# A fused attention and recurrence layer on one core: the score products as 32-row strips of four heads, without the copies that stacked them

## The chip, the cores and the metric

The kernel runs on one core of a Trainium2 chip. The time is device microseconds of one execution, the median of several runs. A second, profiled execution gives the span from the first to the last instruction and the rows that are quoted. "PE" is the matrix engine (TensorE), "PEld" its loads of stationary weights, DVE, ACT and POOL are the vector, scalar and GpSimd engines, and SP is the engine whose queue issues nearly all transfers (SPq in rows).

## The reference

512 tokens of 1024 features go through one layer. A vector `c` gives shift, scale and gate; then

```
h    = rmsnorm(x) * (1 + scale) + shift
proj = h @ w_in                       # q, k, v, z_attn, x_lru, z_lru
q, k = rope(q), rope(k)               # 8 heads of 64
s    = (q @ k.T) / 8, causal          # MoBA: 2 blocks of 256, top 3, so all past blocks are kept
attn = softmax(s) @ v
rec  = rg_lru(causal_conv(x_lru))     # recurrence over time
y    = [rmsnorm(attn) * silu(z_attn), rmsnorm(rec) * silu(z_lru)] @ w_out
out  = rmsnorm(x + gate * y) * final_gain
```

Everything is float32. The kernel gets near that accuracy with operands split into a rounded high part and a low part (`hi`, `lo`, type fp32r) and three products: hi·hi, hi·lo and lo·hi.

## The kernel before

**Order.** The whole program is written as a list of operations (`op`), each with an engine, an estimated cost, the tiles it reads and writes, and a due time. `Plan.emit` (line 97) simulates the engines with these estimates, picks the next operation of each engine, and so fixes one order for each engine and for SP's transfer queue. On the chip each engine runs its order as it stands: an instruction whose input is late holds up all that stand behind it on that engine. Tiles come from pools of `N2` buffers of 2 KB per partition, `N4` of 4 KB and `N8` of 8 KB (line 182) and from 8 banks of PSUM, of which at most 6 are given to `"side"` work at a time (scores, transposes, gates); a load waits until a buffer of its pool is free. `after` on an operation holds it back to a planned time.

**Stages.** (1) Opening: `x` is loaded in four tiles `xt[t]`, scaled by its rms on ACT and DVE, first the 128 columns `xs[t]` that the first transposes need (line 332), then the rest (line 344, held back by `REST[t]`). The modulation weights `wss` are multiplied with `cb` on DVE to give the gain and shift `g` of each 128 features (`gain`, line 367; those of d = 0 come as four tiles of 128x512, line 285, each read from rows 8 KB apart). A 16-column transfer `touch` of `wss` is issued ahead on ACT's queue (line 276). (2) For d = 0 to 7, PE transposes `x`, ACT writes `h` and its high part, and 21 products go into seven banks `acc` (line 420). This gives q and k of heads 0 to 3 and three channel blocks of the recurrence. (3) The other columns follow as units (`UNITS`, line 31), each 24 products of 128x512 (`mm3`, lines 242 to 244), with the recurrence, the gates and the attention planned in between. (4) The output projection goes over `g` = 0 to 3 (half of the features, first for the recurrence, then for attention) and four token tiles, and the final norm of each token tile follows its last product.

**Attention.** The columns of q and k are ordered so that a rotary tile `hi[32*s + i, j, token]` holds features 32j to 32j+31 of head s of a group of four: 32 rows for each head, in two halves j. `rope` (line 452) makes `hi` and `lo` of a group. Then `stack` (line 473) copies them with transfers: for each pair of heads p it builds `q..s` (rows 0 to 63 the high part, 64 to 127 the low part of one head), `k..hs` (the high part twice) and `k..ls` (the low part twice), four transfers for each tile, on SP's queue with a planned latency `MOVE`. `attend(p, i)` (line 564) makes the scores of token tile i for the two heads of a pair with four products over all 128 rows, n = 128(i+1) columns each:

```
for s in range(2):
    for part in range(2):
        PE.matmul(ps[s][:, :n], q[:, s, m], ks[part][:, s, :n], start=part == 0, stop=part == 1)
```

For each head DVE takes the row minimum while it copies the scores from PSUM (line 581), ACT takes the exponent (line 584), PE transposes it (`transposed`, line 612) and a copy brings it to `pt`. After i = 3 the pair's products with v follow (`av`, line 596; two heads in two column strips of 64), and its normalisation. There are 16 calls of `attend`, `SPACE` = 7.5 planned us apart.

**End.** The last token tile is cut into two halves of 256 columns (line 766). For every cut, DVE adds to the residual (`xr`, line 778), squares are summed (`o`, line 785 or 789), ACT takes the root (line 801), DVE the reciprocal (line 804), then ACT scales the first half (`oa`, line 809) and DVE the second (`ob`, line 812), and the results are stored by SP (lines 819, 821) and one by ACT's queue (line 816).

Of the kernel before, what the change touches and what calls it, by code (L numbers as in the profile page):

```python
# [7 lines left out]
F32 = mybir.dt.float32  # L8
# [3 lines left out]
OP = mybir.AluOpType  # L12
# [11 lines left out]
REST = (0.0, 12.9, 13.0, 13.1)  # L24
MOVE = 3.4
# [6 lines left out]
SPACE = 7.5  # L32
# [145 lines left out]
def tile_hymba_block(ctx: ExitStack, tc: tile.TileContext, x, wss, wgt, win0, wv, winr,  # L178
# [3 lines left out]
    N2, N4, N8 = 39, 21, 3  # L182
# [91 lines left out]
    touch = fix("touch", [128, 16])  # L274
    op("A", 0.1, lambda: A.dma_start(touch[:], wss[0][:, 0, 0:16]), [], [touch], -100)
# [56 lines left out]
    xs = [Buf("t2", [128, 128], F32, f"xs{t}") for t in range(NT)]  # L332
    xdue = (4.0, 5.0, 6.0, 7.0)
    scr = [t4("scr0"), t4("scr1")]
    for t in range(NT):
# [8 lines left out]
        for dst, cut, e, due2, after in ((xs[t], slice(0, 128), "VVAA"[t], due + 0.4, 0.0), (xt[t], slice(128, D), "A", 20.0 + t, REST[t])):  # L344
# [52 lines left out]
    for d in range(ND):  # L397
        g, xp = gain(d), bank(f"xp{d}")

        def turn(xp=xp, d=d):  # L400
            for t in range(NT):
                PE.transpose(xp[:, t * 128:(t + 1) * 128], xt[t][:, d * 128:(d + 1) * 128], ident[:])  # L402
        if d:
            op("PE", 0.44, turn, xt + [ident], [xp], t_first(d) - (3.8 if d > 1 else 1.6))
        for t in range(NT if not d else 0):
            op("PE", 0.11, lambda t=t, xp=xp: PE.transpose(xp[:, t * 128:(t + 1) * 128], xs[t][:], ident[:]),
# [45 lines left out]
    def rope(pss, kind, group, scale, due):  # L452
# [20 lines left out]
    def stack(p, name, part, other=None):  # L473

        st = t4(f"{name}s", F32R, (128, 2, 512))
        for s in range(2):
            rows = slice(64 * (p % 2) + 32 * s, 64 * (p % 2) + 32 * s + 32)
            for src, to in ((part, slice(0, 64)), (other or part, slice(64, 128))):
                op("SP", 0.5, lambda s=s, src=src, to=to, rows=rows: SP.dma_start(  # L479
                    st[to, s].bitcast(F32), src[rows].bitcast(F32)), [src], [st], None, lat=MOVE)  # L480
        return st
# [413 lines left out]
```

## Time and profile before

| | |
|---|---|
| median of 3 runs | 242.12 us (241.91 to 245.52) |
| profiled execution, its own time | 243.68 us |
| its span, first to last instruction | 241.9 us |
| PE busy | 229.6 us (95%), 1123 matmuls |
| DVE busy | 198.4 us (82%) |
| ACT busy | 142.5 us (59%) |
| transfers | 44.29 MB, 15231 packets |

The busy time of an engine counts an instruction from its start to its end; matmuls overlap, so the time that one adds to a row of matmuls is read from the chain of waits, not from the duration of one. "Idle before" a row is the engine's own idle time, with what ended it.

### The profile page before, as it was taken

The numbers are of one execution on the slowest core, as the hardware profiler recorded it, in microseconds if no ns is written. First come the engines' busy times: TensorE is split into PE (matmuls) and PEld (weight loads), VectorE is DVE, ScalarE is ACT, GpSimd is POOL, SyncE is SP. The second block draws the span as 40 slices with busy tenths as digits, with TensorE's granted clock in tenths as the row PEclk, the third lists the DMA queues.
The fourth block names the chain that finished last, engine by engine and source line by source line (L and its number), as shares of the span: only waits on it lengthen the run. The fifth ranks groups of instructions, "written<-read, shape, count | busy, mean of one in ns | idle before, by whom it ended". The sixth has DMA issues, their size and how long they took to land.

```text
span 241.9 us, 3282 instructions
## 1 busy us (share of the span) xinstructions
PE 229.6 (95%) x1123; PEld 183.0 (76%) x1123; DVE 198.4 (82%) x367; ACT 142.5 (59%) x262; POOL 11.6 (5%) x32
## 2 busy tenths in 40 slices
PE   7959999999999979999999999999999999999990
PEld 4348888888888858788888688786888868888880
DVE  3399999989448979997799989998999998626473
ACT  7885645557225096439899999583554755003362
POOL 1000000038600000000000000000000000000000
PEclk9999999999999999999999999999999999999997
DMA  6999999913799947054079896292430100000045
GB/s 203 323 412 413 413 414 414 408 51 87 177 280 207 294 173 226 38 173 173 0 177 322 205 293 221 75 360 90 154 107 16 72 3 0 0 0 0 3 158 189
DMA packets 15231, 44.29 MB, mean 183 GB/s; under 512 B 2288, under 2 KB 2928, under 8 KB 14576
## 3 DMA queue, kind: packets, MB, share of 16 engines
q1 hardware_dynamic: 14928, 43.96, 54.6%
q8 instruction: 9, 0.15, 0.3%
q10 hardware_dynamic: 288, 0.14, 0.2%
q14 instruction: 6, 0.05, 0.1%
HBM read 35.70 MB, written 2.10 MB: 156 GB/s over the span
## 4 chain that ended last, share of the span: by engine, by line
PE 78%; DMA 9%; SPq 4%; DVE 3%; ACT 2%; issue 1%; ACTq 0%
PE acc L420 16%; PE pj L242 10%; PE pj L244 9%; PE pj L243 9%; PE po L242 6%; PE po L244 6%; PE po L243 6%; PE av L596 4%; PE sc L573 4%; DMA w<-in_win_dram 4%; PE tp L617 3%; DMA wc<-in_winr_dram 3%; DMA k1hs<-k0h 3%; SPq L239 2%; SPq L479 2%; PE xp L402 1%
## 5 line engine op out<-in xcount | busy, mean ns | idle before, releaser
L584 ACT ACTIVATE z<-z,mn 128x128 f32<-128x128 f32 (+3 forms) x32 | 17.8, 557 | 8.5 <-DVE mn L581 8.5
L581 DVE CUSTOM_DVE_ANT_0 z<-sc,cst 128x128 f32<-128x128 f32 (+3 forms) x32 | 14.7, 485 | 6.7 <-PE sc L573 6.6
L386 DVE SCALAR_TENSOR_TENSOR ws<-ws,cb 128x1024 f32<-128x1024 f32 x14 | 16.9, 1222 | 0.1
L232 ACT COPY pt<-tp 128x128 f32<-128x128 f32 (+3 forms) x28 | 10.0, 408 | 11.1 <-PE tp L617 11.0
L617 PE MATMUL tp<-ident,z 128*128 128x128 f32 x80 | 12.5, 274 | 1.6 <-ACT z L584 1.6
L617 PEld LDWEIGHTS tp<-ident,z 128*128 128x128 f32 x80 | 9.7, 140 | 5.0 <-ACT z L584 2.8
L789 ACT ACTIVATE o<-xr 128x512 f32<-128x512 f32 x7 | 4.4, 633 | 11.8 <-DVE xr L778 11.8
L778 DVE SCALAR_TENSOR_TENSOR xr<-po,rba,xr 128x512 f32<-128x512 f32 (+1 forms) x9 | 6.2, 691 | 6.3 <-PE po L244 6.2
L309 PE MATMUL spare<-warm 128*128 128x512 bf16 x31 | 9.4, 448 | 1.5 <-DVE warm L307 1.5
L498 DVE SCALAR_TENSOR_TENSOR xc<-xl,vec,xc 128x511 f32<-128x511 f32 (+2 forms) x12 | 8.9, 742 | 1.8 <-ACT xc L494 1.7
L778 DVE SCALAR_TENSOR_TENSOR xr<-po,rbl,xr 128x512 f32<-128x512 f32 x8 | 6.0, 750 | 5.0 <-PE po L244 4.6
L544 DVE SCALAR_TENSOR_TENSOR wgt<-wgt,cb 128x1024 f32<-128x1024 f32 x8 | 9.7, 1216 | 0.0
L761 DVE TENSOR_TENSOR wo<-wo,grow 128x1024 f32<-128x1024 f32 x8 | 9.7, 1211 | 0.0
L596 PE MATMUL av<-pt,v 128*64 128x512 f32 (+3 forms) x64 | 9.5, 439 | 0.0
L596 PEld LDWEIGHTS av<-pt,v 128*64 128x64 f32 x64 | 4.2, 136 | 5.3 <-issue 4.6
L309 PEld LDWEIGHTS <-warm 128*128 128x128 bf16 x31 | 3.6, 118 | 5.1 <-issue 1.8
L743 ACT ACTIVATE rba<-ss,epsc 128x4 f32<-128x4 f32 x1 | 0.3, 263 | 10.8 <-PE ss L741 10.8
L639 ACT ACTIVATE sz<-pj 128x512 f32<-128x512 f32 x8 | 4.8, 594 | 3.1 <-PE pj L244 3.0
L409 ACT ACTIVATE h<-xp,g 128x512 f32<-128x512 f32 x8 | 6.1, 768 | 0.0
L584 ACT ACTIVATION_READ_ACCUMULATOR z<-z,mn 128x1 f32 x32 | 6.0, 188 | 0.0
L640 DVE SCALAR_TENSOR_TENSOR sz<-sz,pj 128x512 f32<-128x512 f32 x8 | 5.4, 678 | 0.3 <-ACT sz L639 0.3
L232 ACT COPY rc<-rs 128x512 f32<-128x512 f32 x3 | 1.8, 587 | 6.6 <-PE rs L606 6.6
(1121 smaller groups left out, 772.3 us busy)
## 6 DMA issues: line engine op xcount, KB each, us to landing
wc<-in_winr_dram SPq DMA_DIRECT2D x13, 512.0 KB, 5.5
ws<-in_wss_dram SPq DMA_DIRECT2D x4, 1024.0 KB, 11.9
wgt<-in_wgt_dram SPq DMA_DIRECT2D x8, 512.0 KB, 5.0
wo<-in_wo_dram SPq DMA_DIRECT2D x8, 512.0 KB, 3.7
w<-in_win_dram SPq DMA_DIRECT2D x7, 448.0 KB, 8.6
ws<-in_wss_dram SPq DMA_DIRECT2D x6, 512.0 KB, 7.8
x<-in_x_dram SPq DMA_DIRECT2D x4, 512.0 KB, 5.4
wv<-in_wv_dram SPq DMA_DIRECT2D x4, 512.0 KB, 8.8
```

The source lines that it names most:

```text
L232: op("A", acp(n) if psum else ac(n), lambda: A.copy(dst(), src()), r, w, due, after=after, alt=("V", dv(n) if psum else dv2(n), lambda: V. ...
L242: PE.matmul(ps, lh, rh, start=start, stop=False)
L243: PE.matmul(ps, lh, rl, start=False, stop=False)
L244: PE.matmul(ps, ll, rh, start=False, stop=stop)
L309: op("PE", 0.32 if n < 11 else 0.235, lambda: PE.matmul(spare[:], warm[:, 0:128], warm[:], start=True, stop=True), [warm], [spare], 5.3 + ...
L386: op("V", dv(1024), lambda j=j: V.scalar_tensor_tensor(part(d, j), part(d, j), 1.0, cb[:], op0=OP.mult, op1=OP.mult, accum_out=sc[:, j:j + ...
L420: PE.matmul(acc[j][:], w[:, k * 128:(k + 1) * 128], b[:], start=first, stop=last),
L581: op("V", dv(n) + 0.085, lambda s=s, z=z: V.tensor_tensor_reduce(out=z[:, :n], in0=ps[s][:, :n], in1=cst[:, 2048 - n:2048], op0=OP.add, op ...
L584: op("A", ac(n, 1, 1), lambda s=s, z=z: A.activation(z[:, :n], z[:, :n], AF.Exp, bias=mn[s][:, 0:1], scale=-1.0, accum_out=sm[:, i, s:s + ...
L596: PE.matmul(ps2[64 * s:64 * s + 64, k * 128:], vt[k][:, (2 * p + s) * 64:(2 * p + s + 1) * 64], pts[s][:, k, k * 128:], start=(k == 0), st ...
L617: PE.transpose(tp[:, k * 128:(k + 1) * 128], z[:, k * 128:(k + 1) * 128], ident[:])
L778: op("V", dv(w, 1), lambda t=t, ps=ps, c0=c0, c1=c1, br=br: V.scalar_tensor_tensor(res[t][:, c0:c1], ps[:, :c1 - c0], rb[br][:, t:t + 1], ...
```

## The change

Five things change.

- **Scores.** `stack` and its transfers go. `attend(group, i)` now takes four heads at once: for each of three pairs of parts (hi·hi, hi·lo, lo·hi) and two halves j, four products follow each other, one for each head, each over the 32 rows of that head in the rotary tiles and into that head's own PSUM bank. That is 24 products over 32 rows in place of 8 over 128 rows for the same four heads, and four banks in place of two. The rest for each head is as before, and the products with v move into `attended`.
- **Planned times.** 8 calls of `attend`, 15 us apart, the first at `T_REST + 10` in place of `+ 13`.
- **Pools.** `N2`, `N4`, `N8` go from 39, 21, 3 to 35, 17, 6.
- **Opening.** `touch` goes; the first `wss` block is laid out on the host so that each of its four loads is one contiguous piece (`ws0`); `xs` takes 256 columns, so that the transposes of d = 1 come from it too, and the rest of `x` is held back longer (`REST`).
- **End.** The last token tile is cut 384 + 128. Its second half is multiplied by `fg` ahead of the norm and scaled in place on ACT; both halves are stored whole, the first by SP, the second by ACT's queue. The sum of squares enters the root as its bias.

```diff
-REST = (0.0, 12.9, 13.0, 13.1)
-MOVE = 3.4
+REST = (13.3, 13.4, 17.2, 17.3)
-SPACE = 7.5
+SPACE = 15.0
-    N2, N4, N8 = 39, 21, 3
+    N2, N4, N8 = 35, 17, 6
-    touch = fix("touch", [128, 16])
-    op("A", 0.1, lambda: A.dma_start(touch[:], wss[0][:, 0, 0:16]), [], [touch], -100)
-                    load(ws[d][j][n], wss[0][:, j, 512 * n:512 * n + 512], -97.2 + 0.2 * n - 0.5 * j, kb=256)
+                    load(ws[d][j][n], ws0[j, n], -97.2 + 0.2 * n - 0.5 * j, kb=256)
-    xs = [Buf("t2", [128, 128], F32, f"xs{t}") for t in range(NT)]
+    xs = [Buf("t2", [128, 256], F32, f"xs{t}") for t in range(NT)]
...
-        for p in (2 * group, 2 * group + 1):
-            if kind == "q":
-                QK[f"q{p}"] = stack(p, f"q{p}", hi, lo)
-            else:
-                QK[f"k{p}"] = stack(p, f"k{p}h", hi), stack(p, f"k{p}l", lo)
+        QK[name] = hi, lo
...
-    def attend(p, i, due):
+    def attend(group, i, due):
...
-        ps = [bank("sc", "side") for _ in range(2)]
+        ps = [bank("sc", "side") for _ in range(4)]
         def scores():
-            for s in range(2):
-                for part in range(2):
-                    PE.matmul(ps[s][:, :n], q[:, s, m], ks[part][:, s, :n], start=part == 0, stop=part == 1)
-        op("PE", 4 * pe(n), scores, [q, *ks], ps, due)
+            for c, (a, b, j) in enumerate((a, b, j) for a, b in ((0, 0), (0, 1), (1, 0)) for j in range(2)):
+                for s in range(4):
+                    r = slice(32 * s, 32 * s + 32)
+                    PE.matmul(ps[s][:, :n], q[a][r, j, m], k[b][r, j, :n], start=c == 0, stop=c == 5)
+        op("PE", 6 * max(pe(n), 0.11) + 0.2, scores, [*q, *k], ps, due)
...
-            cuts = (0, 256, 512) if g == 3 and t == NT - 1 else (0, 512)
+            last = g == 3 and t == NT - 1
+            cuts = (0, 384, 512) if last else (0, 512)
...
+                if not n:
+                    to = (outa, outb)[half][t]
+                    op("V", dv(w), lambda t=t, to=to, lo=lo, up=up, c0=c0, c1=c1: V.tensor_mul(
+                        to[:, lo:up], res[t][:, c0:c1], fg[:, c0:c1]), [res[t], fg], [to], t1 + (1.0 if half else 5))
...
+                op("A", 0.2, lambda t=t, q=q: A.activation(ssq[t][:, 3:4], ssq[t][:, q:q + 1], AF.Sqrt,
+                                                           bias=ssq[t][:, 0:1], scale=1.0 / D), [n4], [n4], t1 + 0.3, "sqrt")
...
+                    e = "V" if last and to is outa[t] else "A"
...
+                op("SP", 0.5, lambda t=t: SP.dma_start(out[t * 128:(t + 1) * 128, 0:512], outa[t][:]), [done_a, outa[t]], [], t1 + 2)
+                if last:
+                    op("A", 0.4, lambda t=t: A.dma_start(out[t * 128:(t + 1) * 128, 512:1024], outb[t][:]),
+                       [done_b, outb[t], *more], [], t1 + 2)
```

## Rows read from the trace of the kernel before

**Rows 1.** The page's first part (busy time, share of the span, instructions) and the waits of PE, longest first (engine, line, tile waited with, who ended it; us in total, times, longest).

```profile
PE 229.6 (95%) x1123; PEld 183.0 (76%) x1123; DVE 198.4 (82%) x367; ACT 142.5 (59%) x262; POOL 11.6 (5%) x32
...
PE acc L420 <- ACT h0h L409: 1.7, 1, 1.7
PE tp L617 <- ACT z L584: 1.6, 1, 1.6
```

**Rows 2.** Busy time of the engines in stretches (start:end in us, its length, then busy us and instructions of each engine, the granted PE clock as a share of full speed, the share of the transfer engines, GB/s).

```profile
15.60:84.90 69.30, 69.29 (x325) 57.24 (x325) 59.87 (x106) 34.06 (x52) 10.64 (x25) 1.00 0.85 292
...
86.70:235.60 148.90, 148.85 (x755) 120.33 (x755) 127.76 (x227) 92.91 (x180) 0.00 (x0) 1.00 0.37 118
...
110.00:140.00 30.00, 30.00 (x155) 24.19 (x154) 26.51 (x55) 28.79 (x49) 0.00 (x0) 1.00 0.65 183
```

**Rows 3.** The stall near 85 us: the timeline of ACT and PE, then a piece of the chain of waits (start, us, what) and one row of SP's queue.

```profile
84.26 1.05 ACT L232 CAST wc2h<-wc 128x1024 fp32r<-128x1024 f32 x1 [5.45 <-DMA wc<-in_winr_dram]
...
86.67 1.15 PE L617 MATMUL tp<-ident,z 128*128 128x128 f32 x6 [1.60 <-ACT z L584]
...
76.83 7.33 DMA wc<-in_winr_dram
...
75.80 0.54 SPq L479 DMA_DIRECT2D k1ls<-k0l  x1
```

**Rows 4.** Two of the sixteen groups of stacking transfers (eight of x4, eight of x2: 48 transfers of 128 KB; the last number is the median us from issue to landing).

```profile
k1hs<-k0h SPq DMA_DIRECT2D x4, 128.0 KB, 6.8
...
q3s<-q1l SPq DMA_DIRECT2D x2, 128.0 KB, 3.8
```

**Rows 5.** The chain of waits: the four score products of one pair of heads at n = 512, 128, 256 and 384 (in order of time).

```profile
89.90 0.91 PE sc L573 x4
...
99.20 0.40 PE sc L573 x4
...
115.02 0.47 PE sc L573 x4
...
148.33 0.71 PE sc L573 x4
```

**Rows 6.** Where the array is used in two column strips. First PE's groups with their shapes kept apart (busy us, mean ns of one), a full-array product beside one in strips; then four weight loads of `av` in the timeline, and a line's summary of their durations (min/median/max ns).

```profile
L596 PE MATMUL av<-pt,v 128*64 128x512 f32 x16 | 4.3, 618 | 0.0
...
L420 PE MATMUL acc<-h7h,w07h 128*128 128x512 f32 x7 | 2.4, 389 | 0.0
...
99.53 0.20 PEld L596 LDWEIGHTS av<-pt,v 128*64 128x64 f32 x4
...
L596 PEld LDWEIGHTS av<-pt,v x64: 132/137/137, 99.5 to 198.8; 128*64 128x64 f32 x64
```

**Rows 7.** The chain of waits around `av`: pieces of it ahead of, in and behind it.

```profile
134.16 0.44 PE rs L606 x4
...
163.50 0.28 PE pj L242
...
164.25 2.31 PE av L596 x16
166.55 0.59 PE rs L606 x4
...
199.15 0.43 PE po L242
```

**Rows 8.** The first scores: the timeline of DVE (two rows).

```profile
60.85 1.21 DVE L465 SCALAR_TENSOR_TENSOR q0l<-raq,q0h 128x1024 fp32r<-128x1024 f32 x1
...
67.78 0.29 DVE L581 CUSTOM_DVE_ANT_0 z<-sc,cst 128x128 f32<-128x128 f32 x1 [4.58 <-PE sc L573]
```

**Rows 9.** The opening: GB/s in 40 slices of 0.5 us from 0 to 20 us, then the timeline of DVE, ACT and PE.

```profile
GB/s 0 0 0 55 109 238 385 287 377 418 336 221 336 393 401 401 352 209 147 127 344 356 389 393 412 400 427 432 418 418 409 389 420 398 424 393 418 426 386 412
...
10.79 0.69 DVE L374 SCALAR_TENSOR_TENSOR ws<-ws,cb 128x512 f32<-128x512 f32 x1 [0.74 <-DMA ws<-in_wss_dram]
...
13.85 0.62 ACT L232 CAST w00512h<-w 128x512 fp32r<-128x512 f32 x1 [0.56 <-DMA w<-in_win_dram]
...
14.32 0.16 DVE L384 TENSOR_TENSOR g<-sch,sc 128x1 f32<-128x1 f32 x1
...
14.79 0.77 ACT L409 ACTIVATE h0h<-xp,g 128x512 fp32r<-128x512 f32 x1
...
15.61 1.19 PE L420 MATMUL acc<-h0h,w00512h 128*128 128x512 f32 x4 [1.69 <-ACT h0h L409]
```

**Rows 10.** The end: the timeline behind the last product of PE, and the landing time of the last stores.

```profile
235.65 0.48 DVE L778 SCALAR_TENSOR_TENSOR xr<-po,rba,xr 128x256 f32<-128x256 f32 x1
...
236.17 0.42 DVE L785 SCALAR_TENSOR_TENSOR o<-xr 128x256 f32<-128x256 f32 x1
...
236.52 0.74 DVE L812 SCALAR_TENSOR_TENSOR ob<-xr,ssq,fg 128x512 f32<-128x512 f32 x1
236.64 0.29 ACT L801 ACTIVATE ssq<-ssq 128x1 f32<-128x1 f32 x1 [0.28 <-DVE o L785]
237.18 0.15 DVE L804 RECIPROCAL ssq<-ssq 128x1 f32<-128x1 f32 x1
...
238.33 0.92 SPq L821 DMA_DIRECT2D out_dram<-ob  x2
...
out_dram<-ob SPq DMA_DIRECT2D x2, 128.0 KB, 2.2
```

More of the change, by code (lines that the diff above doesn't have):

```diff
@@ L177, in tile_hymba_block @@
 @with_exitstack
-def tile_hymba_block(ctx: ExitStack, tc: tile.TileContext, x, wss, wgt, win0, wv, winr,
+def tile_hymba_block(ctx: ExitStack, tc: tile.TileContext, x, ws0, wss, wgt, win0, wv, winr,
                      wo, wg, vecs, fgain, consts, out):
@@ new lines, in scores @@
+            for c, (a, b, j) in enumerate((a, b, j) for a, b in ((0, 0), (0, 1), (1, 0)) for j in range(2)):
[3 more added lines that the diff above has]
+        op("PE", 6 * max(pe(n), 0.11) + 0.2, scores, [*q, *k], ps, due)
+        for s in range(4):
+            p, z, mn = 2 * group + s // 2, t2("z"), col("mn")
+            if i == 0 and s % 2 == 0:
+                SUM[p] = fix(f"sum{p}", [128, 4, 2])
+            sm = SUM[p]
+            op("V", dv(n) + 0.085, lambda s=s, z=z, mn=mn: V.tensor_tensor_reduce(
+                out=z[:, :n], in0=ps[s][:, :n], in1=cst[:, 2048 - n:2048], op0=OP.add, op1=OP.min, scale=1.0, scalar=BIG,
+                accum_out=mn[:, 0:1]), [ps[s], cst], [z, mn])
+            op("A", ac(n, 1, 1), lambda s=s, z=z, mn=mn, sm=sm: A.activation(
+                z[:, :n], z[:, :n], AF.Exp, bias=mn[:, 0:1], scale=-1.0, accum_out=sm[:, i, s % 2:s % 2 + 1]),
+               [z, mn], [z, sm], None, "exp")
+            if i == 0:
+                PT[4 * group + s] = Buf("t8", [128, 4, 512], F32, f"pt{4 * group + s}")
+            transposed(z, PT[4 * group + s], i, n, m, due + 0.8 * s)
@@ new lines, in attend, with attended, av, spread @@
+        if i == 3:
+            for p in (2 * group, 2 * group + 1):
+                attended(p, due + 1.6 * (p % 2))
+    def attended(p, due):
+        sm = SUM[p]
+        due += 1.6
+        ps2 = bank("av", "side")
+        pts = [PT[2 * p], PT[2 * p + 1]]
+        def av():
+            for k in range(4):
+                for s in range(2):
+                    PE.matmul(ps2[64 * s:64 * s + 64, k * 128:], vt[k][:, (2 * p + s) * 64:(2 * p + s + 1) * 64],
+                              pts[s][:, k, k * 128:], start=(k == 0), stop=(k == 3))
+        op("PE", 2.2, av, pts + vt, [ps2], due + 7.62)
+        rp, rb4, rc, at = bank("rs", "side"), t2("rb"), t2("rc"), t2("at")
+        op("V", 0.1, lambda: V.reciprocal(sm[:], sm[:]), [sm], [sm])
+        op("A", ac(512), lambda: A.copy(rb4[:].rearrange("p (k s m) -> p k s m", k=4, s=2),
+                                        sm[:, :, :, None].to_broadcast([128, 4, 2, 64])), [sm], [rb4])
+        def spread():
+            for k in range(4):
+                PE.transpose(rp[:, k * 128:(k + 1) * 128], rb4[:, k * 128:(k + 1) * 128], ident[:])
+        op("PE", 0.44, spread, [rb4, ident], [rp], due + 7.7)
+        copy(512, lambda: rc[:], lambda: rp[:], [rp], [rc], None, True)
+        op("V", dv(512), lambda: V.tensor_mul(at[:], ps2[:], rc[:]), [ps2, rc], [at], due + 11)
+        ATT[p] = at
@@ L698, in attend_until @@
         nonlocal done
-        while done < 16 and t_att[done] < t and f"q{att[done][0]}" in QK:
+        while done < 8 and t_att[done] < t and f"q{att[done][0]}" in QK:
             attend(*att[done], t_att[done])
-            p = att[done][0]
-            if p in ATT and p in SZ and ("a", p) not in Y:
-                branch_out("a", p, ATT[p], SZ[p], t_att[done] + 11)
+            for p in (2 * att[done][0], 2 * att[done][0] + 1):
+                if p in ATT and p in SZ and ("a", p) not in Y:
+                    branch_out("a", p, ATT[p], SZ[p], t_att[done] + 13)
             done += 1
```

117 lines of the change are left out of this document (35 added, 82 removed).

## Prediction

> **What bounds the kernel now.** I read the busy times and PE's waits first, then busy time by stretches, then the timeline and the chain of waits at the few places where PE is not busy. PE is the bound: 95% of the span, and in all of it one wait for an input behind the opening [rows 1]. From the first product at 15.6 us to 84.9 us PE is busy in 69.29 of 69.30 us, and from 86.7 to 235.6 us in 148.85 of 148.9 us, at the full granted clock [rows 2]. So the span is four pieces: 15.6 us until the first product, 218.3 us of PE's queue, a hole of 1.6 to 1.8 us, and 6.3 us behind the last product (235.6 to 241.9). A change moves the time by what it does to one of these four; work on other engines and transfers count only where they make PE wait. DVE is the next bound: 26.51 of 30 us from 110 to 140 [rows 2].
>
> **The scores on PE.** Before, the four products of a pair took 0.40, 0.47, 0.71 and 0.91 us at n = 128, 256, 384, 512 [rows 5], or 0.100, 0.118, 0.178 and 0.228 for one; four pairs make 4 x 2.49 = 9.96 us. Now there are 24 products over 32 rows for four heads at each n. A product takes as long over 32 rows as over 128 unless strips work side by side: its time in [rows 5] goes with the columns, down to 0.100 at n = 128. So two ends.
> - Four strips at once: six steps, 6 x (0.100 + 0.118 + 0.178 + 0.228) = 3.74 us for a group, 7.5 for both.
> - One after another: 24 x 0.624 = 15.0 us for a group, 30.0 for both.
>
> No row shows row strips. The nearest shows column strips: `av` uses two of 64 columns. Its record at 512 columns lasts 618 ns; a full-array record of 389 ns advances the queue by about 0.23 us (0.91 / 4 in [rows 5]), so 0.16 us of a record is not its own. 16 x (0.618 - 0.16) = 7.3 us of own work stand in 4.3 us of busy time: a factor of 1.7, near 2. Weight loads are side by side there too: four, of 0.137 us each, within 0.20 us [rows 6]. I take four strips at once, because the only strips in this trace work like that.
>
> Strips cost something when the array changes over. Ahead of `av` the product at 163.50 takes 0.28 instead of 0.23 us, behind it four transposes take 0.59 instead of 0.44, or one product 0.43 instead of 0.23 [rows 7]. That is 0.05 + 0.15 to 0.20, so 0.25 us for a visit; 8 visits, 2.0 us. Sum: 7.5 + 2.0 - 9.96 = **-0.4 us**; at the other end 30.0 + 2.0 - 9.96 = **+22.0 us**. The work for each head behind the scores (minimum, exponent, transposes, copies, products with v) keeps its counts, so it costs nothing new.
>
> The Trainium skill ("TensorE: Matmul & The Clock Gate", Part 3) gives 3.07 times, not 4, for four row strips at 512 columns; by it, as an estimate, the 30.0 us would become 9.8 and the term +1.8. This case's trace shows no row strips; its column strips gave 1.7 of 2, which would speak for the smaller factor too. "TensorEngine Tiling (Array Packing)", Key Properties, says that changing the mode drains the array; the 0.25 us of [rows 7] agrees.
>
> **The stacking transfers.** 48 transfers of 128 KB leave [rows 4], 6.3 MB of 44.29. Issuing one holds SP's queue for about 0.54 us [rows 3], some 26 us in all, and they wait for `hi` and `lo` while loads stand behind them. That is what made the hole at 85 us: ACT waits 5.45 us for weights `wc2`, issued at 76.83 behind a stacking transfer and 7.33 us under way; the exponents stand behind that on ACT, and PE's transposes wait 1.60 us for them [rows 3]. Without the transfers the load is issued earlier and meets less traffic: **-1.6 us**, down to 0 if the smaller pool `N4` (17 for 21) makes the load wait for a buffer instead. The other stalls of SP cost PE nothing now, as PE has no other wait.
>
> The first scores no longer wait for transfers. `q0l` is ready at 62.1 us, while DVE sat 4.58 us until 67.78 for scores [rows 8]; so they come some 4 us earlier. But they now follow `q0l` directly in the plan, with little between, and PE is in order: if DVE is 0.5 us later than planned PE stands still that long, with projection products queued behind. Four banks at a time also bind two thirds of the six for side work; a late DVE then holds PE on the next bank, where before two were needed, and DVE has 3.5 us of slack in 30 [rows 2]. Between 0 and 3 us; I take **+0.4 us**, near the low end, as the same planner left only one such wait in 149 us behind 86.7.
>
> **The opening.** The first product waits for `h0h` [rows 1], which needs `g` (ready 14.48) and stands behind `w00512h`, whose weights came at 13.85; both follow the transfers. These run at about 400 GB/s, but from 8.5 to 10 us at 209, 147 and 127, just ahead of the wait of DVE for the first `ws` tile at 10.79 [rows 9]. Three slices at 161 instead of 400 GB/s lost 0.9 us. The rows don't say whether the 8 KB stride or a first reading of this memory is the reason. If the stride is, contiguous `ws0` gives 0.9 back; if the removed `touch` was what kept the other three tiles fast, each of those may lose as much, +2.7. Scaling of the wide rest of `x` moves behind `h0h`, and ACT was waiting for weights there in any case (0.56 us), so this gives 0 to 0.3 us: `h0h` started 0.3 us after `g`. `xs` doubled costs under 0.2 us on ACT and DVE, in the same wait. I take **-0.3 us**, from -1.2 to +2.7.
>
> **The end.** Cutting 384 + 128 adds PE time: 12 x (0.178 + 0.100) = 3.34 us instead of 24 x 0.118 = 2.83 [rows 5], +0.5. Behind PE, from [rows 10]: before, `xr` (256 columns, 0.48) from 235.65, `o` 0.42, root, then the reciprocal at 237.18, held up by an `ob` of the tile before, and the two last stores issued one behind the other, the second at about 238.8, so 3.2 us after PE; the last store lands 2.2 us later. Now: `xr` and `o` of 128 columns, by 0.133 us less each, 0.35 and 0.29; root 0.29 and reciprocal 0.15, with hand-overs 1.25 us; then on DVE 512 columns (0.4 to 0.75) and 128 (0.35) beside ACT's 384 (0.6), and two stores from two queues: the last issued about 2.2 us after PE. That saves 1.0, at worst nothing: DVE also has `xr`, `o` and the product with `fg` of the 384 columns (0.61 + 0.55 + 0.5) to do within the 1.2 us of the last 12 products. Net **-0.4 us**, from -0.6 to +0.6.
>
> **Sum.** -0.4 - 1.6 + 0.4 - 0.3 - 0.4 = -2.3 us on the profiled span: 241.9 becomes 239.6. The profiled execution itself took 243.68, 1.8 more than its span and 1.6 more than the median; taking the 2.3 off the median gives 242.1 - 2.3 = **239.8 us**, 1.0% faster.
>
> **Rivals.**
> - *The gains are eaten.* The hole only moves (a load waits for one of 17 buffers, +1.6), PE waits on banks or on `q0l` (to +3 in place of 0.4), the strips reach 3 of 4 (30.0 / 3 + 2.0 - 9.96 = +2.0 in place of -0.4). One or two of these give 241.5 to 246. For: DVE near its limit, fewer buffers. Against: SP has less to issue, and DVE gets its first scores 4 us earlier.
> - *Strips work one after another.* The other side: +22.0 in place of -0.4, so 242.1 + 20.1 = 262 us; with products side by side but weight loads in turn, 0.100 each (the floor at n = 128), a call takes at least 2.4 us, 19.2 + 2.0 - 9.96 = +11.2, so 251. Pairs at once give 15.0 + 2.0 - 9.96 = +7, 247. PE has no slack to hide it. It decides from a step of four products that takes 0.2 us more than one product: 48 steps make 10 us. Against: the column strips of [rows 6].
> - *Everything helps.* Opening -1.2, end -0.6, hole -1.6, no new wait, scores -0.4, and DVE's earlier start: -3.8 to -5.2, so 237 to 238.3.
> - *The change doesn't do what it says:* the load is late for another reason and the hole stays. Then 241.4, inside the first rival.
>
> **Chances.** Forecast (238.3 to 241.5) 0.44; gains eaten (241.5 to 246) 0.26; all helps (236.8 to 238.3) 0.14; strips not four at once (246 and more) 0.16. The range 236.8 to 246 holds 0.84; the likeliest case alone is 238.3 to 241.5. 2% is 4.8 us, about what a measurement of this kernel can tell from no change (its three runs differ by 3.6 us): faster than 237.3 takes nearly all the gains, 0.07; slower than 246.9, from strips in turn, 0.15; between, 0.78.
>
> **What the profile will show.** Four score products starting within a few hundredths of a us of each other, and a call at n = 512 moving PE's queue by about 1.6 us (right), 2.5 (loads in turn) or 5.5 (products in turn). No wait of ACT for `wc2` of several us and no PE wait near 85 us; PE waits elsewhere with DVE or ACT named would be the first rival. The first product ahead of 15.6 us, and 209, 147, 127 gone from the GB/s row, or not. About 5.3 us between PE's last product and the end. The prediction is wrong if PE's queue from first to last product is longer than 218 us, or has waits that sum to over 2 us.

## The result and the profile after

The changed kernel takes 240.57 us (median of 20 runs, 239.91 to 240.91), the kernel before 242.18 in the same comparison (20 runs, 241.29 to 246.50): ratio 0.991, 95% interval 0.9891 to 0.9928. The medians are 1.6 us apart, and the spread shrank from 5.2 to 1.0 us. The ratios here and below are the record's estimates from the executions that lie no more than 1.5% above their kernel's fastest, while medians and ranges are of all executions, so a ratio need not be the quotient of two medians. The profiled execution after took 240.57 like its median, the one before 243.68, 1.5 above its own. So the two profiles differ by 3.0 us, two typical runs by about half of that.

| piece of the span, us | before | forecast | after |
|---|---|---|---|
| until the first product | 15.6 | 15.3 | 14.3 |
| PE from the first to its last product, without the hole | 218.3 | 218.9 with what is left of the hole | 218.7 |
| hole near 85 us | 1.7 | (in the line above) | 0 |
| behind the last product | 6.3 | 5.4 (5.3 among the forecast's marks) | 5.9 |
| span | 241.9 | 239.6 | 238.9 |

First the busy times and then all waits of PE in the changed kernel, to be held against [rows 1]:

```profile
PE 230.0 (96%) x1251; PEld 180.7 (76%) x1251; DVE 201.9 (85%) x375; ACT 133.7 (56%) x251; POOL 8.8 (4%) x32
...
PE spare L306 <- DVE warm L304: 1.5, 1, 1.5
PE acc L417 <- ACT h0h L406: 1.0, 1, 1.0
PE xp L403 <- DVE xs L348: 0.3, 1, 0.3
PE acc L417 <- DVE h0l L408: 0.2, 1, 0.2
```

Behind the opening no wait of PE is left from before, neither for `z` near 85 us nor for a score, a bank or `q0l`. The one new wait is `h0l`, 0.2 us. Busy times by stretches (columns as in [rows 2]): the opening, PE's queue, the end.

```profile
10.00:15.00 5.00, 3.98 (x20) 2.09 (x21) 4.42 (x17) 4.07 (x11) 0.00 (x0) 1.00 1.01 359
14.30:232.90 218.60, 218.39 (x1204) 174.91 (x1204) 192.23 (x342) 120.78 (x226) 7.87 (x25) 1.00 0.41 149
232.90:239.00 6.10, 0.08 (x1) 0.00 (x0) 2.02 (x10) 1.79 (x4) 0.00 (x0) 0.68 0.46 172
```

**Scores.** The chain of waits at the calls of the first group, n = 128 to 512 (start, length, what; a count under 24 says only that the chain passed fewer of the call's records), most with the projection product behind it; then PE's timeline of the call at n = 512, which has all 24.

```profile
64.98 0.82 PE sc L558 x24
65.81 0.43 PE pj L241
...
96.48 0.92 PE sc L558 x24
97.39 0.43 PE pj L241
...
105.38 1.28 PE sc L558 x21
...
108.92 1.60 PE sc L558 x22
110.52 0.44 PE pj L241
```

```profile
108.85 0.74 PE L558 MATMUL sc<-k0h,q0h 32*128 32x512 f32 x8
109.42 0.64 PE L558 MATMUL sc<-k0l,q0h 32*128 32x512 f32 x8
109.87 0.65 PE L558 MATMUL sc<-k0h,q0l 32*128 32x512 f32 x8
110.45 0.51 PE L241 MATMUL pj<-h6h,wc3h 128*128 128x512 f32 x1
```

24 products of 512 columns pass in 1.60 us: the forecast's first mark for four strips at once. The rows show it more closely: from 109.42 to 109.87 us two steps, eight products, take 0.45 us, 0.225 for a step of four, as long as the 0.228 of one full-array product before. The trace's single records agree: the first four products start within 0.01 us. What a call takes beyond six such steps belongs to the visit: 1.60 - 6 x 0.228 = 0.23 us at n = 512, 0.82 - 6 x 0.100 = 0.22 at n = 128. And the product behind a call takes 0.43 us where its neighbours take 0.23. Both groups together take 9.2 us in the calls (4.62 and 4.60) and 8 x 0.2 = 1.6 behind them: 10.8, against 9.96 by the forecast's rows of the calls before. So the term is +0.8 by these rows; PE's whole queue gives less (below).

**The load of `wc2`.** ACT's cast and the row of SP's queue that issues the load, which answer to [rows 3]:

```profile
77.98 1.05 ACT L231 CAST wc2h<-wc 128x1024 fp32r<-128x1024 f32 x1
```

```profile
70.04 0.33 SPq L238 DMA_DIRECT2D wc<-in_winr_dram  x1
```

The load is issued at 70.04 in place of 76.83, the cast runs 6.3 us earlier, and no idle time stands before it. The loads of this kind also land sooner (DMA issues before, then after: KB each, median us to landing):

```profile
wc<-in_winr_dram SPq DMA_DIRECT2D x13, 512.0 KB, 5.5
```

```profile
wc<-in_winr_dram SPq DMA_DIRECT2D x13, 512.0 KB, 3.4
```

Transfers fell from 15231 packets and 44.29 MB to 10960 and 38.01.

**Opening.** The GB/s row of the first 20 us in 40 slices, then rows of the timeline (an engine's own idle time in brackets), which answer to [rows 9]:

```profile
GB/s 0 0 0 50 130 188 410 418 410 418 352 369 393 385 401 361 385 393 389 393 410 414 380 394 324 262 254 369 401 384 438 443 409 423 402 418 429 397 434 415
```

```profile
13.04 0.16 DVE L381 TENSOR_TENSOR g<-sch,sc 128x1 f32<-128x1 f32 x1
...
14.28 1.21 PE L417 MATMUL acc<-h0h,w00512h 128*128 128x512 f32 x4 [1.02 <-ACT h0h L406]
...
17.99 1.21 PE L417 MATMUL acc<-h0l,w00512h 128*128 128x512 f32 x4 [0.21 <-DVE h0l L408]
```

The 209, 147 and 127 are gone, and `g` is ready 1.3 us earlier. Of the 1.3 us that the first product gained, 0.4 is lost again: from there to the first product with `h0l` it is 3.71 us, 3.31 before (15.61 to 18.92, the row below).

```profile
18.92 0.41 PE L420 MATMUL acc<-h0l,w00512h 128*128 128x512 f32 x1
```

What the opening is worth is better read at the end of the stage of `acc`. The first product of the units starts at 55.98 us, before at 57.21: 1.2 us earlier. The profiles of the six other kernels below with the same or nearly the same opening start their first product anywhere from 14.15 to 14.87 us, and all leave this stage between 55.5 and 56.1.

**End.** The timeline from PE's last product on, which answers to [rows 10], and the DMA issue of the last store (KB each, us to landing):

```profile
232.70 0.28 PE L243 MATMUL po<-wo31h,ya3l 128*128 128x128 f32 x1
...
232.86 0.55 DVE L785 TENSOR_TENSOR ob<-xr,fg 128x384 f32<-128x384 f32 x1
233.33 0.34 DVE L770 SCALAR_TENSOR_TENSOR xr<-po,rba,xr 128x128 f32<-128x128 f32 x1
...
234.38 0.16 DVE L798 RECIPROCAL ssq<-ssq 128x1 f32<-128x1 f32 x1 [0.36 <-ACT ssq L796]
...
235.40 0.37 ACTq L815 DMA_DIRECT2D out_dram<-ob  x1
```

```profile
out_dram<-ob ACTq DMA_DIRECT2D x1, 256.0 KB, 2.4
```

PE is done at 232.98, but the last `xr` starts at 233.33, behind the 384-column work on DVE; before, it started 0.04 us after PE's last product (235.61 and 235.65). The last store is issued 2.4 us after PE in place of 3.2, then takes 2.4 us to land in place of 2.2.

### The profile page after: what moved, and what is told of

The parts are those of the page before. It is cut to its first block, busy times and chain, and to the rows that moved or that the text cites. A ratio compares the mean times of both kernels' runs of the same rounds, so it can differ in the third digit from the quotient of the medians.

```text
span 238.9 us, 3458 instructions
## 1 busy us (share of the span) xinstructions
PE 230.0 (96%) x1251; PEld 180.7 (76%) x1251; DVE 201.9 (85%) x375; ACT 133.7 (56%) x251; POOL 8.8 (4%) x32
## 2 busy tenths in 40 slices
DMA packets 10960, 38.01 MB, mean 159 GB/s; under 512 B 1344, under 2 KB 1472, under 8 KB 10304
## 4 chain that ended last, share of the span: by engine, by line
PE 89%; DMA 6%; DVE 2%; SPq 1%; issue 0%; ACT 0%; DVEq 0%
PE acc L417 15%; PE pj L241 14%; PE pj L243 13%; PE pj L242 13%; PE po L241 6%; PE po L243 6%; PE po L242 6%; PE av L587 4%; PE sc L558 4%; PE tp L608 4%; DMA ws<-in_wss_dram 3%; DMA x<-in_x_dram 3%; PE xp L399 1%; PE rs L597 1%; SPq L238 1%; PE ss L732 1%
## 5 line engine op out<-in xcount | busy, mean ns | idle before, releaser
L770 DVE SCALAR_TENSOR_TENSOR xr<-po,rba,xr 128x512 f32<-128x512 f32 (+2 forms) x9 | 6.2, 690 | 6.1 <-PE po L243 6.0
L231 ACT COPY pt<-tp 128x128 f32<-128x128 f32 (+3 forms) x21 | 7.8, 410 | 2.6 <-PE tp L608 2.6
L232 DVE COPY pt<-tp 128x384 f32<-128x384 f32 (+3 forms) x11 | 5.6, 526 | 2.5 <-PE tp L608 2.3
L517 DVE TENSOR_TENSOR_SCAN th<-gr,gi 128x512 f32<-128x512 f32 x4 | 4.9, 1221 | 0.1
```

Of the source, the lines that this page charges most:

```text
L770: op("V", dv(w, 1), lambda t=t, ps=ps, c0=c0, c1=c1, br=br: V.scalar_tensor_tensor(res[t][:, c0:c1], ps[:, :c1 - c0], rb[br][:, t:t + 1], ...
```

## The experiments

The theory after the result: the four terms add up, with the hole (a load behind SP's stacking transfers) and the contiguous first weights as the two that count. The rivals: each gain belongs to another edit, or a gain alone isn't there because something else takes it back.

### The parts alone: scores, opening, end

The scores with their planned times and pools, put into the kernel before:

```diff
-MOVE = 3.4
-SPACE = 7.5
+SPACE = 15.0
-    N2, N4, N8 = 39, 21, 3
+    N2, N4, N8 = 35, 17, 6
...
-    def attend(p, i, due):
+    def attend(group, i, due):
...
+        ps = [bank("sc", "side") for _ in range(4)]
```

> The kernel before with the new scores, their planned times and the pools alone; opening and end as before. My theory: the hole of PE near 85 us (1.6 to 1.8 us) goes with the stacking transfers and the strips cost PE about what the stacked products did, so about 1.6 us less than before (240.6 against 242.2), with the first product at about 15.6 us. Rival (the hole depends on when the opening ends, and the gain is the opening's): the hole or one like it stays, and the time is within 0.5 us of before.

Measured: 242.06 us (241.44 to 243.76), before on that chip 243.27, ratio 1.000 (0.9968 to 1.0032). The hole is gone, yet by the ratio the time is the same: the expectation missed. Three views (ACT's cast of `wc2`, two stretches of busy time, PE's first products) say what took it back:

```profile
77.89 1.05 ACT L231 CAST wc2h<-wc 128x1024 fp32r<-128x1024 f32 x1 [4.04 <-DVE wc1l L249]
```

```profile
10.00:15.00 5.00, 2.45 (x12) 0.85 (x10) 3.87 (x16) 3.30 (x9) 0.00 (x0) 1.00 1.05 402
...
15.50:20.00 4.50, 4.50 (x13) 3.58 (x14) 4.45 (x10) 3.41 (x4) 0.00 (x0) 0.62 1.03 408
```

```profile
15.49 2.01 PE L419 MATMUL acc<-h0h,w00512h 128*128 128x512 f32 x4 [1.60 <-ACT h0h L408]
```

The cast comes as early as in the changed kernel and waits for no load. But behind the first product the granted clock falls from 2.4 to 1.2 GHz, 0.62 of full speed as the mean of 4.5 us: the first four products take 2.01 us, 1.21 at the full clock. From the first product to the end of the stage of `acc` it is 43.2 us in place of 41.6, so 1.6 us. For the other executions only the mean granted clock of the whole is known, as a share of full speed. In 5 of these 12 it was 0.984 to 0.986 (243.03 to 243.76 us), in 7 it was higher (241.44 to 242.08). That is not the scores' doing, as the kernel before has both kinds too: 9 of 27 executions in this comparison at 0.984 to 0.987 (median 243.46), 18 above (242.3). I take a low mean for such a fall, as the two profiles of this first series with a low mean (this one and the end alone) show it there; where it fell in the other executions no profile shows. Above, the new scores give 241.77 against 242.3, so 0.5 us, within the scatter of those before (241.11 to 244.12); below, 243.35 against 243.46.

The opening alone, and the end alone:

```diff
-REST = (0.0, 12.9, 13.0, 13.1)
+REST = (13.3, 13.4, 17.2, 17.3)
-    op("A", 0.1, lambda: A.dma_start(touch[:], wss[0][:, 0, 0:16]), [], [touch], -100)
-                    load(ws[d][j][n], wss[0][:, j, 512 * n:512 * n + 512], -97.2 + 0.2 * n - 0.5 * j, kb=256)
+                    load(ws[d][j][n], ws0[j, n], -97.2 + 0.2 * n - 0.5 * j, kb=256)
-    xs = [Buf("t2", [128, 128], F32, f"xs{t}") for t in range(NT)]
+    xs = [Buf("t2", [128, 256], F32, f"xs{t}") for t in range(NT)]
```

> The kernel before with the new opening alone (contiguous first block, no early touch, 256 columns first, the rest of x held back). My theory: the first product starts about 1.3 us earlier (14.3 in place of 15.6 us), of which 0.3 to 0.4 is given back at the first low part of h, and the hole near 85 us stays: about 1 us less than before (241.2). Rival (the earlier start is lost again at the hole, since the loads behind it are no earlier): the hole grows by as much and the time is as before (242.2).

```diff
-            cuts = (0, 256, 512) if g == 3 and t == NT - 1 else (0, 512)
+            last = g == 3 and t == NT - 1
+            cuts = (0, 384, 512) if last else (0, 512)
```

> The kernel before with the new end alone. My theory after the trace of after: 0.3 to 0.6 us more products on PE, and 0.4 us less behind the last product, so within 0.3 us of before. Rival (the prediction's term): 0.4 us less than before.

Measured: the opening 241.70 (ratio 0.9967, 0.9938 to 0.9996), the end 242.53 (0.9991, 0.9958 to 1.0024). Both are within 0.5 us of what was expected, the end by the ratio. With the opening alone the first product starts at 14.15, no execution of 12 has a low mean clock, and PE still waits near 85 us (first fence, waits of PE). With the end alone the profiled execution has the fall (second fence, a stretch), which cost 2.8 us this time (44.4 us in place of 41.6 to the end of the stage of `acc`), and no wait of PE near 85 us.

```profile
PE tp L615 <- ACT z L582: 0.8, 1, 0.8
```

```profile
15.00:20.00 5.00, 4.63 (x11) 3.67 (x12) 4.96 (x10) 3.78 (x5) 0.00 (x0) 0.50 1.03 409
```

So the kernel before loses time at two places, and in this profile one hides the other: where the fall makes PE late, ACT's late cast (still 4.03 us of waiting for the load) no longer holds it up. That `wc2` comes late doesn't always cost 1.6 us either: it cost 0.8 with the opening alone. By the ratios the parts alone gain 0.0, 0.3 and 0.1%, each within about 0.3, and all together 0.9%. The sum is smaller than the whole, but not clear of it by these intervals, so the runs don't show that the parts need each other.

### Which edit of the opening

Three kernels, each the kernel before with one edit: the first weights contiguous (the order of each engine stays as it is); `touch` removed; `xs` doubled with `REST`.

```diff
-                    load(ws[d][j][n], wss[0][:, j, 512 * n:512 * n + 512], -97.2 + 0.2 * n - 0.5 * j, kb=256)
+                    load(ws[d][j][n], ws0[j, n], -97.2 + 0.2 * n - 0.5 * j, kb=256)
```

> The kernel before with the first wss block laid out contiguously, and nothing else; the early touch stays (it now reads a block that no other load reads). Every engine keeps its order. Theory (the 8 KB stride makes the slow stretch from 8.5 to 10 us): that stretch goes, and the first product starts about 1 us earlier, at 14.5 to 14.8 us, without the fall of the granted clock behind it. Rival (a first reading of this memory, or the touch, makes it): GB/s still fall to about 150 near 9 us and the first product stays at 15.4 to 15.6 us.

```diff
-    touch = fix("touch", [128, 16])
-    op("A", 0.1, lambda: A.dma_start(touch[:], wss[0][:, 0, 0:16]), [], [touch], -100)
```

> The kernel before without the early touch, the loads as before. Theory (the touch is worth nothing): first product at 15.4 to 15.6 us, the slow stretch near 9 us as before. Rival (the touch costs the later loads something, or kept them fast): the slow stretch is gone or is longer, and the first product is 0.5 us or more earlier or later.

```diff
-REST = (0.0, 12.9, 13.0, 13.1)
+REST = (13.3, 13.4, 17.2, 17.3)
-    xs = [Buf("t2", [128, 128], F32, f"xs{t}") for t in range(NT)]
+    xs = [Buf("t2", [128, 256], F32, f"xs{t}") for t in range(NT)]
```

> The kernel before with 256 columns scaled first and the rest of x held back, and nothing else. Theory: the first product waits for transfers, so it moves by at most 0.3 us; the transposes of d = 1 fill PE before it, so the granted clock falls in fewer executions than in the kernel before, where it does so in about 4 of 10. Rival (ACT's order was what held the first product up): first product 0.5 us or more earlier.

Measured: 241.74 (ratio 0.9941, 0.9905 to 0.9977), 243.18 (1.0021, 0.9980 to 1.0063), 242.49 (0.9988, 0.9950 to 1.0026). The GB/s rows of the first 20 us and the first product, contiguous; then without `touch` the GB/s row and ACT's cast of `wc2`:

```profile
GB/s 0 0 0 47 142 262 336 393 393 410 311 246 393 418 393 406 389 397 418 397 393 406 385 415 385 327 246 352 410 446 407 407 430 409 442 410 421 417 415 414
```

```profile
14.64 1.21 PE L420 MATMUL acc<-h0h,w00512h 128*128 128x512 f32 x4 [1.49 <-ACT h0h L409]
```

```profile
GB/s 0 0 0 49 99 238 352 369 401 418 352 270 352 434 401 418 262 131 111 131 365 402 385 393 409 396 439 419 451 401 409 396 417 403 399 410 451 393 390 419
```

```profile
82.14 1.06 ACT L232 CAST wc2h<-wc 128x1024 fp32r<-128x1024 f32 x1 [3.66 <-DMA wc<-in_winr_dram]
```

The layout removes the slow stretch and brings the first product from 15.61 to 14.64. So neither `touch` nor a first reading of the memory makes it: `ws0` is read for the first time too. `touch` does nothing that can be seen: the stretch is there without it (131, 111, 131), in the same place. Without `touch` the load of `wc2` was issued at 76.08 and under way 6.1 us in place of 7.3, and PE didn't wait at all, though no line about the stacking differs: the hole varies from one execution to the next. `xs` with `REST` keeps PE busy 3.44 of the 5 us before 15 in place of 2.92 (row below) and shows no low mean clock in its executions, but gains no time that can be measured.

```profile
10.00:15.00 5.00, 3.44 (x17) 1.60 (x17) 4.17 (x16) 3.17 (x9) 0.00 (x0) 1.00 1.05 405
```

By the profiles, the stage of `acc` ends at 56.29 with the layout alone, 57.04 without `touch`, and 56.71 with `xs` and `REST`, against 57.21 before: 0.9, 0.2 and 0.5 us. A mean clock of 0.988 or less stands in 2 of 10, 4 of 10 and 0 of 10 executions, and in 11 of 24 of the kernel before. That speaks for `xs` with `REST` as what keeps the fall away, but ten executions of one kernel don't show it; and the layout alone, expected to run without it, had it in two.

### Strips in turn

The changed kernel, with the loops over heads and steps exchanged, so that a head's six products follow each other:

```diff
-            for c, (a, b, j) in enumerate((a, b, j) for a, b in ((0, 0), (0, 1), (1, 0)) for j in range(2)):
-                for s in range(4):
+            for s in range(4):
+                for c, (a, b, j) in enumerate((a, b, j) for a, b in ((0, 0), (0, 1), (1, 0)) for j in range(2)):
```

> The changed kernel with one line exchanged for its neighbour: the loop over the four heads is outside and that over the six steps inside, so the same 24 products follow each other strip by strip. My theory: strips work side by side only where neighbours in the queue use different strips; now a call takes about 24 times 0.107, 0.113, 0.17 and 0.228 us, the eight calls together some 21 to 23 us more than the 9.2 us they take in the changed kernel, and the time is about 262 us. Rival (the four strips are filled whatever the order, or a product over 32 rows is cheap by itself): the time stays at 240.6 us.

Measured: 250.44 (ratio 1.0339, 1.0278 to 1.0400), chain and timeline of the call at n = 512:

```profile
112.18 3.31 PE sc L558 x23
```

```profile
112.11 0.73 PE L558 MATMUL sc<-k0h,q0h 32*128 32x512 f32 x2
112.68 0.39 PE L558 MATMUL sc<-k0l,q0h 32*128 32x512 f32 x1
112.69 0.49 PE L558 MATMUL sc<-k0h,q0h 32*128 32x512 f32 x1
112.91 0.39 PE L558 MATMUL sc<-k0l,q0h 32*128 32x512 f32 x1
...
113.15 0.38 PE L558 MATMUL sc<-k0h,q0l 32*128 32x512 f32 x1
```

The order of the queue is what puts the strips side by side: 9.9 us for one exchange of loops. But the call at n = 512 takes 3.31 us, twice the interleaved one and not four times, so the expected 262 us missed as well. The rows show why. The first row holds both `k0h,q0h` steps of the first head. At 112.69 the first step of the next head starts, 0.01 us after the first head's third step (`k0l,q0h`, 112.68), and ahead of that head's fourth and fifth, which stand before it in the queue and start at 112.91 and 113.15. So a product for a free strip starts while earlier ones of a busy strip still wait: here PE does not run its order strictly as it stands. As an estimate, 24 x 0.228 = 5.5 us of products in 3.31 us are 1.7 side by side.

### What makes the hole

In the kernel before, the stacking transfers issued by POOL in place of SP; in the changed kernel, the same 48 transfers added without use, on SP and on POOL:

```diff
-                op("SP", 0.5, lambda s=s, src=src, to=to, rows=rows: SP.dma_start(
+                op("G", 0.5, lambda s=s, src=src, to=to, rows=rows: G.dma_start(
```

> The kernel before with the stacking transfers issued from POOL's queue in place of SP's; the same 48 transfers. Theory A (SP's order makes the hole: the loads stand behind transfers that wait for rotary tiles): wc2 is issued earlier and lands before ACT needs it, no wait of PE near 85 us. Theory B (the traffic makes it: 6.3 MB more in the same stretch): wc2 is under way for about 7 us as before and the hole of 1 to 2 us stays.

```diff
+        for p in (2 * group, 2 * group + 1):
+            for part, other in (((hi, lo),) if kind == "q" else ((hi, hi), (lo, lo))):
+                st = t4(f"{name}s", F32R, (128, 2, 512))
...
+                        op("SP", 0.5, lambda st=st, s=s, src=src, to=to, rows=rows: SP.dma_start(
+                            st[to, s].bitcast(F32), src[rows].bitcast(F32)), [src], [st], T_REST + 8 + 64 * group + 30 * (p % 2), lat=3.4)
```

> The changed kernel with the 48 stacking transfers put back on SP's queue, into buffers that nothing reads; scores, opening and end stay as changed. Theory A (SP's order or the traffic of the transfers makes the hole near 85 us): weights land late again, ACT waits for them for several us, and PE waits 0.5 to 2 us; about 1 to 2 us more than the changed kernel (241.5 to 242.5). Theory B (the hole came from the scores' own wait for the stacked copies): no wait of PE, and the time stays within 0.5 us of 240.6.

> The same idle transfers, but from POOL's queue, so that they add traffic and SP's queue holds loads alone. If SP's order is the cause: loads are issued as in the changed kernel, no hole, within 0.5 us of 240.6. If the traffic is: as with the transfers on SP.

Measured: 247.32 (ratio 1.0175, 1.0110 to 1.0240), 250.49 (1.0337, 1.0259 to 1.0416), 256.50 (1.0581, 1.0490 to 1.0672). One long wait of each: of PE, of ACT (the last number of its timeline's row) and of DVE:

```profile
PE sc L573 <- DMA q0s<-q0l: 1.4, 1, 1.4
```

```profile
82.00 1.05 ACT L231 CAST wc2h<-wc 128x1024 fp32r<-128x1024 f32 x1 [5.41 <-DMA wc<-in_winr_dram]
```

```profile
DVE wc1l L249 <- DMA q0s<-q0l: 10.5, 1, 10.5
```

By time none of the three separates the causes, and none came out within its expectations. In the first, from POOL, the scores wait for the copies (1.4 us), and the load of `wc2` is issued at 81.24, later than from SP. Its profile also has the fall of the clock behind the first product (the stretch is shown in the last section), which cost 1.6 us, and a second one at 74 us. In the other two the copies hold buffers of the pool of 4 KB, and DVE waits for one of these (`wc1l`, 10.5 us, with the copies on POOL).

In one respect the last two do say something. The copies on SP's queue bring the late load back into the changed kernel: ACT waits 5.41 us for `wc2`, as in the kernel before. From the issue of the load of `wc1` to that of `wc2` it is 10.2 us there (67.09 to 77.26) and 9.4 in the kernel before (67.46 to 76.83), but 7.0 with the copies on POOL (67.19 to 74.16) and 7.0 in the changed kernel (63.04 to 70.04). So copies in SP's queue are enough to put 2 to 3 us between these two loads. What the traffic and the buffers add stays open: these loads land after a median of 5.5 us with the copies on SP, 4.2 with them on POOL and 3.4 without, and `wc1` is 4 us late with either. Nor do the three show how much of the 1.6 us of PE each made; 48 such copies can cost far more.

### Two mends

The changed kernel with its end mended (the last half scaled in one DVE step, the first on ACT), and with that and `h0l` ahead of the second gain product of d = 1 on DVE:

```diff
-                if not n:
+                if not n and not (last and half):
...
-                    op("V", dv(w, 1), lambda t=t, lo=lo, c0=c0, c1=c1: V.scalar_tensor_tensor(
+                    op("V", dv(512, 1), lambda t=t: V.scalar_tensor_tensor(
```

> The changed kernel with less on DVE in the last token tile: the second half is not multiplied by the gain ahead of the norm but in one step behind it (128x512, 0.75 us), beside ACT, which scales the first half. Theory (the 384-column product with the gain holds up the last addition by 0.5 us, which ate the saving of the end): the span behind PE's last product falls from 6.2 to 5.6 or 5.8 us, and the time by 0.4 to 0.5 us to about 240.1. Rival (the stores and what follows them set the end whatever DVE does): no change.

```diff
-               [ws[d][j], cb], [ws[d][j], sc])
+               [ws[d][j], cb] + ([hl[0]] if d == 1 and j == 0 else []), [ws[d][j], sc])
```

> As the run before, and the low part of the first h is made on DVE ahead of the second product with the modulation weights of d = 1, so that PE need not wait for it at 17.7 us (0.37 us between two products beyond the usual 0.23). Theory: another 0.3 us less, about 239.8. Rival (the products of d = 1 then wait for their gain as long): as the run before, or the planned order behind it shifts and costs more.

Measured: 240.44 (ratio 0.9901, 0.9867 to 0.9935), not to be told from the changed kernel, and 243.73 (1.0052, 1.0018 to 1.0086). The first, in its timeline and its DMA issues:

```profile
233.02 0.35 DVE L770 SCALAR_TENSOR_TENSOR xr<-po,rba,xr 128x128 f32<-128x128 f32 x1
...
235.04 0.37 ACTq L814 DMA_DIRECT2D out_dram<-ob  x1
```

```profile
out_dram<-ob ACTq DMA_DIRECT2D x1, 256.0 KB, 2.7
```

The last store is issued 0.36 us earlier and lands in 2.7 instead of 2.4 us. The store of the first half was issued at 235.01, in place of 235.09; counted from there, the last store lands after 2.7 us in both (235.04 + 2.7, 235.40 + 2.4). The profiles with the old order of the last steps (end alone, strips in turn) have 2.4 too, the one with both mends 2.7. So the landing of the two stores, and not DVE's work before the second, sets the end. This execution also started its first product at 14.87, 0.6 later than the changed kernel's, was only 0.18 later at the first product with `h0l`, and level at the first scores (64.98): the last half microsecond of the opening was worth nothing here. The second has no wait for `h0l`, but the plan came out differently behind it (the load of `wc2` at 73.33 in place of 70.04), and PE waits elsewhere (row below). In 6 of its 12 executions the mean granted clock was 0.984 or 0.985; where the clock was low in these, no profile shows.

```profile
PE pj L243 <- DVE wc9l L249: 2.2, 1, 2.2
```

No kernel tried is clearly faster than the changed one.

## Why the prediction was right, point by point

The forecast was 239.8 us for the median and came out 0.8 low, inside its range and on its side of "within 2%". The mechanisms were mostly right, but several sizes were off and cancelled. On the profiled span the terms measured -1.2 for the opening (forecast -0.3), about -0.2 for the scores and the rest of PE's queue (-0.4), nothing for first scores and banks (+0.4), -1.7 for the hole (-1.6) and +0.1 for the end (-0.4): -3.0 in place of -2.3. That the sum came as near as that is in part luck.

- *PE is the bound, and the time is four pieces.* Right: each microsecond is found in one of the four.
- *Scores, -0.4.* Four strips at once: right, and strips in turn cost 9.9 us, so the order matters. The size of a step was right too, 0.225 us at n = 512 for 0.228. The size of a visit was not: 0.2 us inside the call and 0.2 behind it, 0.43 where the step took 0.25, 1.4 us more over 8 visits. By the calls the term is +0.8. By PE's queue it is smaller: 218.3 before; less 0.44 for the four transposes of d = 1, which moved ahead of the first product; plus 0.5 at `h0l` and 0.5 for the cut of the end: 218.9, and 218.7 were measured, so -0.2 is left for the scores and all else. Most of the difference can be assigned by counting, behind the stage of `acc`, from the start of each product to the start of the next. The score calls took 10.4 us before, more than the 9.96 of the rows, and 9.2 after; the projection products take 1.7 more without the hole, nearly all of it the 8 x 0.2 behind the calls; and the transposes of `z` 0.5 less (7.5 and 6.9). So the scores themselves cost about 0.5 us more, and cheaper transposes, which no step had and no run explains, hide it. The Trainium skill ("TensorE: Matmul & The Clock Gate", Part 3) gives 3.07 times for four row strips. The runs show more: 24 products in series would be 24 x 0.228 = 5.5 us, so 1.60 with both changes of mode is 3.4 times, and the eight products in 0.45 us between them are 4.0 times (8 x 0.228 = 1.82).
- *The hole, -1.6.* Gone, and the load is issued 6.8 us earlier, as the step says. As a size it held for the profiled execution alone. In kernels that keep the stacking it was 0.8, 0.7 or nothing, so on the median the term is smaller. That the new scores, with their times and pools, remove the late load is shown by the scores alone (cast at 77.89). That the copies in SP's queue are enough to bring it back is shown by the run that adds them (5.41 us of ACT's waiting); what part SP's order, the traffic and the buffers each had in it three runs did not settle.
- *First scores and banks, +0.4.* Not there: no wait of PE for any of them. DVE had 192 us of work in 218.6 and came in time. The first scores start 2.5 us earlier (64.91, before 67.41), not 4. And the step's reason for the low end misreads [rows 2]: behind 86.7 us there was no wait at all.
- *The opening, -0.3.* The contiguous layout was worth 0.97 at the first product, as in the step's "0.9 back"; the doubt about `touch` was void. The term was mis-sized: in place of -0.3 it was -1.3 at the first product and -0.44 for the four transposes moved ahead of it, less 0.5 lost to `h0l`, so -1.2, as at the end of the stage. What is late next, `h0l`, the step had left out.
- *The end, -0.4.* The PE part was +0.5, as forecast (the 24 products took 2.87 us before and 3.39 after), the part behind PE -0.4 in place of -1.0, so +0.1 net. The step's own doubt came true: DVE's 384-column work holds the last `xr` for 0.3 us (233.33, and 233.02 with the end mended). And mending that gave nothing, as two stores of 256 KB together take longer to land.
- *From profile to median.* Taking the whole 2.3 off the median was the choice that made the number 0.8 low: the profile lost 3.0, the medians 1.6. The profile before held a hole larger than in the other profiles that keep the stacking.
- *Its own sign of being wrong.* "PE's queue from first to last product is longer than 218 us" came true: 218.7. The sign was set wrong, as the queue before already took 218.3 and the forecast's terms add 0.5 to it. The other sign, waits of over 2 us, did not come: 0.2.

What neither the forecast nor a rival had: the clock fall at the first product, by the mean granted clock in a third of the executions before. The changed kernel shows none in 20 (mean granted clock 0.991 to 0.997); which of the opening's edits keeps it away was not tried alone often enough to say. That accounts for a part of the smaller spread only: the 18 executions before with a higher clock still spread over 3.0 us, the 20 of the changed kernel over 1.0.

## What to carry to other kernels

Two losses that lie one behind the other in an engine's queue can hide each other, as one profile here shows: measure an edit alone and with its neighbours before calling it worthless, and read a wait from several executions, not from one profile. Products over 32 rows filled the array here where neighbours in the queue use different strips, but each visit cost about 0.4 us, so make visits few and long. When an edit brings the first product forward, look at once for the second operand, which was hidden until then.

## What the hardware did that was not expected

- Products overtook across strips: with strips in turn, the call at n = 512 took 3.31 us, neither 5.5 (in series) nor 1.60. The Trainium skill ("TensorE: Matmul & The Clock Gate", Part 3) has matmuls start in program order; the rows from 112.69 to 113.15 show the next head's first step ahead of this head's fourth and fifth.
- Pieces of 2 KB that lie 8 KB apart came at 131, 111 and 131 GB/s in the first tile read, and at about 390 in the next three of the same stride. Contiguous, the first tile came at full rate too (389 to 418). An earlier small read of the same memory made no difference. Why only the first tile was slow the runs don't show.
- The granted clock fell from 2.4 to 1.2 GHz close to the first product in three profiles: with the scores alone 0.1 us behind its start, with the end alone 0.7 ahead of it, with the stacking copies on POOL 0.7 behind it. The loss was 1.6, 2.8 and 1.6 us. PE had been busy for 2.45, 2.51 and 2.92 of the 5 us from 10 to 15 us there. The profile before has 2.92 too, and no fall. So what decides it the runs don't show. The third profile's two stretches:

```profile
10.00:15.00 5.00, 2.92 (x13) 1.19 (x13) 4.01 (x16) 3.91 (x10) 0.00 (x0) 1.00 1.04 402
15.00:20.00 5.00, 4.60 (x13) 3.69 (x14) 4.96 (x10) 3.81 (x5) 0.00 (x0) 0.66 1.03 410
```
